# Three to four residual buffers and a post-norm traced in two parts, in a fp32 trunk of two layers

## The chip, the cores and the metric

The kernel runs on one core of one Trainium2 chip. The metric is the device time of one execution in microseconds. The times of the kernel before are 2248.75, 2250.59 and 2251.07 us, median 2250.59.

## The reference

A sequence of 1024 tokens of width 1024 passes through two layers in float32. The first has an attention mixer (eight banded softmax heads and eight stick-breaking heads), the second a gated linear recurrence. Every layer ends with a SwiGLU feed-forward part (FFN) of inner width 2816, and every sub-layer is wrapped in two RMS norms:

```python
def rmsnorm(x, g):
    y = x * lax.rsqrt(jnp.mean(x * x, axis=-1, keepdims=True) + RMS_EPS)
    return y * g
def swiglu(h, w_gate, w_up, w_down):
    return (jax.nn.silu(h @ w_gate) * (h @ w_up)) @ w_down
# each sub-layer f (mixer, FFN):
x = x + rmsnorm(f(rmsnorm(x, g_pre)), g_post)
```

Both mixers end in a product with a 1024 x 1024 matrix, `... @ w_out`.

## The kernel before

Tokens are handled in eight row blocks of 128. PE (the matrix engine) multiplies in float32 by splitting each operand into a high and a low part and adding three products. ACT (scalar engine) makes the high part by a cast, DVE (vector engine) the low part by a subtraction. POOL computes the small per-row numbers of the norms, SP issues the DMAs in the order of its queue. The program is written stage by stage; the framework's scheduler then fixes the order of every engine's instructions at build time, and each engine runs its list in that order. `issue_after(x)` adds the condition that an instruction is placed after x. It takes the data's own dependences for granted, and the buffers too: a tile with `bufs=n` shares n places, and its next user waits until the oldest one is done.

The stages, in order: attention, the output projection of the attention layer, its FFN in two stages (`gate_up`, `down`), the recurrent mixer, its output projection, and again `gate_up` and `down`.

**Output projection** (`out_product`). Row blocks 0 to 2, then 3 to 5 are summed in six PSUM banks over the eight slices of the inner dimension (L462 is its matmul). Then blocks 6 and 7 follow one by one. Each block's result goes through `norm`: `post_norm` squares the two halves of the PSUM result on ACT (L175 in `rstd`), POOL makes the factor rs from the sums (L177 adds the halves, L178 scales and adds eps, L179 takes the power -1/2), DVE multiplies by the gain (L223) and adds the result to the residual x (L226). The new x is stored, and `pre_norm` makes the next stage's input: square x (L175), factor, scale (L200, ACT), eight transposes on PE (L208, into tiles `pst`), and `take` of `HiddenS`, which copies (L85) and casts (L96) the transposed block and forms its four sums (L89).

**`gate_up`** multiplies the normed input by the gate and up matrices in Strassen form: seven products (`A11`, `A12`, `S2`, `S3`, `S1`, `S4`, `A22`) of half-size operands (L549 to L551 are its three matmuls). The weights' operands `q` are split in `load` (L529, L530; sums at L536 to L542). The very first Strassen product is done in two halves: `early`, columns of row blocks 0 to 3, while blocks 5 to 7 are still being normed, and `late` for blocks 4 to 7. L566 is the copy of the first product.

**`down`** multiplies by the down matrix in a similar form: sums p1, p6, p7, p5, p4, whose operands are loaded in pairs (`raw`) and split at L624/L625 (L629 to L631 are its matmuls). With p4 the second half of the rows (r = 1) is complete, and its four blocks are normed while p3 and then the `b21` products run (their activations `act` are cast at L740, their weights come from L731). The first half's blocks (r = 0) are normed last. In the last layer these post-norms write the output.

## Time and profile before

| | |
|---|---|
| median of three runs | 2250.59 us |
| the profiled execution | 2252.08 us |
| its span in the trace | 2250.3 us |
| PE busy | 2204.5 us (98%) |
| DVE busy | 1537.2 us (68%) |
| ACT busy | 1146.9 us (51%) |
| POOL busy | 220.5 us (10%) |
| mean granted PE clock | 0.992 |

The stages by the trace, with PE's busy time in each:

| stage | from, us | to, us | PE busy, us |
|---|---|---|---|
| attention | 0 | 495 | 486.13 |
| output projection, attention layer | 495 | 609 | 113.53 |
| `gate_up` 0 | 609 | 1015 | 401.08 |
| `down` 0 | 1015 | 1262 | 241.42 |
| recurrent mixer | 1262 | 1500 | 234.67 |
| output projection, recurrent layer | 1500 | 1588 | 87.53 |
| `gate_up` 1 | 1588 | 1990 | 398.03 |
| `down` 1 | 1990 | 2250.3 | 242.09 |

Busy time of an engine is the time in which one of its instructions runs; a stretch in which PE is idle or runs at a lower granted clock is time that the kernel could lose. Times in the trace are counted from the span's start.

### The profile page before, as it was taken

What the parts mean: (1) busy time and instruction counts of PE and PEld (TensorE: products, weight loads), DVE (VectorE), ACT (ScalarE), POOL (GpSimd) and SP (SyncE); (2) the same over time, 40 slices, a digit from 0 to 9 for tenths busy, and PEclk for the clock granted to TensorE, in tenths of its full rate; (3) what the DMA queues carried; (4) which work ended last, traced back from release to release, by engine and by line L of the source; (5) the groups of instructions that cost most, each with busy time, mean ns of one, the idle gap of its engine ahead of it and who ended that gap; (6) DMA issues with size and microseconds to landing.
All of it is one profiled execution on the core that took longest, in us unless ns stands there. A gap on an engine that the chain in (4) does not pass through costs nothing. (4 is left out here: it accounts for less than half of the span.)

```text
span 2250.3 us, 30764 instructions
## 1 busy us (share of the span) xinstructions
PE 2204.5 (98%) x11166; PEld 1804.5 (80%) x11166; DVE 1537.2 (68%) x2504; ACT 1146.9 (51%) x2132; POOL 220.5 (10%) x474
## 2 busy tenths in 40 slices
PE   8999999999999999999999999999999999999997
PEld 8888888878678888888887777887788888888875
DVE  5776765464677767676867677436887767769665
ACT  4545455465765454432536576537755454425433
POOL 2111212131100000000001232102000000000010
PEclk9999999999999999999999999999999999999998
DMA  5101011125623323245558511358233323337466
GB/s 171 44 29 34 24 43 46 55 98 156 223 85 113 116 90 122 89 131 183 173 157 255 141 57 47 95 183 273 71 117 108 122 90 116 96 117 264 130 206 187
DMA packets 187132, 273.13 MB, mean 121 GB/s; under 512 B 13922, under 2 KB 115298, under 8 KB 186979
## 3 DMA queue, kind: packets, MB, share of 16 engines
q1 hardware_dynamic: 186338, 269.06, 38.1%
q10 hardware_dynamic: 640, 2.10, 0.3%
q8 instruction: 88, 1.44, 0.3%
q14 instruction: 66, 0.53, 0.1%
HBM read 205.57 MB, written 65.54 MB: 120 GB/s over the span
## 5 line engine op out<-in xcount | busy, mean ns | idle before, releaser
L549 PE MATMUL ps<-hS,q 128*128 128x512 f32 (+1 forms) x1288 | 490.5, 382 | 3.0 <-ACT hS L96 2.9
L550 PE MATMUL ps<-hS,q 128*128 128x512 f32 (+1 forms) x1288 | 490.6, 381 | 0.2 <-DVE hS L89 0.2
L551 PE MATMUL ps<-hS,q 128*128 128x512 f32 (+1 forms) x1288 | 489.1, 381 | 0.0
L530 DVE TENSOR_TENSOR q<-raw,q 128x512 fp32r<-128x512 f32 x308 | 204.4, 686 | 180.8 <-ACT q L529 180.4
L549 PEld LDWEIGHTS ps<-hS,q 128*128 128x128 f32 x1288 | 242.8, 189 | 50.1 <-ACT hS L96 4.1
L550 PEld LDWEIGHTS ps<-hS,q 128*128 128x128 f32 x1288 | 243.7, 189 | 47.2 <-DVE hS L89 0.7
L551 PEld LDWEIGHTS ps<-hS,q 128*128 128x128 f32 x1288 | 243.6, 189 | 45.8
L529 ACT CAST q<-raw 128x512 fp32r<-128x512 f32 x308 | 176.9, 615 | 157.3 <-DVE raw L538 137.1
L630 PE MATMUL ps<-o,o 128*128 128x512 f32 x616 | 241.2, 392 | 2.4 <-DVE o L625 2.3
L631 PE MATMUL ps<-o,o 128*128 128x512 f32 x616 | 238.6, 392 | 0.5 <-DVE o L741 0.5
L629 PE MATMUL ps<-o,o 128*128 128x512 f32 x616 | 222.0, 395 | 8.9 <-ACT o L740 5.9
L518 ACT ACTIVATE raw<-raw,gcol 128x256 f32<-128x256 f32 x352 | 150.2, 498 | 157.2 <-DMA raw<-in_ffn_w_up_dram 83.1
L624 ACT CAST o<-raw 128x512 fp32r<-128x512 f32 x206 | 123.9, 621 | 197.2 <-PE ps L631 60.5
L625 DVE TENSOR_TENSOR o<-raw,o 128x512 fp32r<-128x512 f32 x206 | 137.9, 688 | 66.2 <-ACT o L624 65.2
L178 POOL TENSOR_SCALAR rs<-ss 128x1 f32<-128x1 f32 x64 | 30.2, 472 | 1266.5 <-ACT junk L175 1169.1
L629 PEld LDWEIGHTS ps<-o,o 128*128 128x128 f32 x616 | 116.4, 189 | 37.7 <-ACT o L740 8.0
L155 DVE TENSOR_TENSOR wlo<-raw,whi 128x1024 fp32r<-128x1024 f32 x76 | 92.9, 1223 | 67.5 <-ACT whi L154 66.4
L630 PEld LDWEIGHTS ps<-o,o 128*128 128x128 f32 x616 | 116.4, 189 | 28.0 <-DVE o L625 3.9
L631 PEld LDWEIGHTS ps<-o,o 128*128 128x128 f32 x616 | 116.3, 189 | 24.9 <-DVE o L741 0.9
L154 ACT CAST whi<-raw 128x1024 fp32r<-128x1024 f32 x76 | 79.8, 1052 | 53.0 <-PE ps L166 20.2
L369 ACT COPY pt<-tr 128x512 f32<-128x512 f32 (+1 forms) x128 | 65.5, 527 | 78.9 <-PE tr L365 78.3
L165 PE MATMUL psq<-hT,whi 128*128 128x512 f32 x256 | 101.2, 395 | 1.1 <-DVE v L264 1.1
(194 smaller groups left out, 4281.1 us busy)
## 6 DMA issues: line engine op xcount, KB each, us to landing
raw<-in_ffn_w_down_dram SPq DMA_DIRECT2D x96, 256.0 KB, 4.3
raw<-in_ffn_w_gate_dram SPq DMA_DIRECT2D x44, 512.0 KB, 4.2
raw<-in_ffn_w_up_dram SPq DMA_DIRECT2D x44, 512.0 KB, 4.4
gS<-c SPq DMA_DIRECT2D x88, 256.0 KB, 3.7
raw<-gS SPq DMA_DIRECT2D x88, 256.0 KB, 2.9
gA<-c SPq DMA_DIRECT2D x66, 256.0 KB, 3.3
raw<-in_attn_w_in_dram SPq DMA_DIRECT2D x24, 512.0 KB, 4.1
raw<-in_attn_w_out_dram SPq DMA_DIRECT2D x24, 512.0 KB, 4.2
```

The source lines that it names most:

```text
L165: nc.tensor.matmul(ps, wh[:, kt, cols], hh[:, kt, :], start=kt == 0, stop=False)
L518: nc.scalar.activation(raw[:, i], raw[:, i], AF.Copy, scale=gain[:, 4 * k + i:4 * k + i + 1])
L529: self.last = nc.scalar.copy(t[:, 0], src).ins
L530: nc.vector.tensor_tensor(t[:, 1], src, t[:, 0].bitcast(F32), op=ALU.subtract)
L549: nc.tensor.matmul(ps, a[:, 0, kt, :], bh, start=kt == 0, stop=False)
L550: nc.tensor.matmul(ps, a[:, 0, kt, :], bl, start=False, stop=False)
L551: nc.tensor.matmul(ps, a[:, 1, kt, :], bh, start=False, stop=kt == 3)
L624: nc.scalar.copy(t[:, 0], src)
L625: tt(t[:, 1], src, t[:, 0].bitcast(F32), op=ALU.subtract)
L629: nc.tensor.matmul(ps, a[0], b[:, 0], start=first, stop=False)
L630: nc.tensor.matmul(ps, a[0], b[:, 1], start=False, stop=False)
L631: nc.tensor.matmul(ps, a[1], b[:, 0], start=False, stop=last)
```

## The change

Four things change.

1. The residual tile x has three buffers instead of two in the output projections and the first `down`. The last `down` takes it from a pool of its own, `late`, with four. In the output projection block 5's x lies in a tile that the first activations also use, and the other activations have two buffers instead of three.
2. `post_norm` is split: a first part (load of x, squares, factor, multiplication by the gain) and a rest (residual, store, pre-norm, transposes). In the output projection the first parts of three blocks are written ahead of their rests, and likewise for blocks 6 and 7.
3. `rstd` scales inside the square and adds eps to the first half's sum, so that one POOL operation less follows the second half's square.
4. Placement: block 6's `take`, and three of the splits for the first gate matrix, are placed after block 7's last square and multiplication (`last_m`). The S2 product of the early half is placed after block 6's last transpose (`turned[6]`), its A22 product after block 7's (`turned[7]`).

```diff
 def rstd(self, pool, parts, junk):
-        for p, o in zip(parts, ss):
-            self.squared = nc.scalar.activation(junk, p, AF.Square, accum_out=o).ins
-        if len(parts) == 2:
-            nc.gpsimd.tensor_tensor(ss[0], ss[0], ss[1], op=ALU.add)
-        nc.gpsimd.tensor_scalar(rs, ss[0], 1.0 / D, EPS, op0=ALU.mult, op1=ALU.add)
+        eps = EPS
+        for i, (p, o) in enumerate(zip(parts, ss)):
+            self.squared = nc.scalar.activation(junk, p, AF.Square, scale=D ** -0.5, accum_out=o).ins
+            if i < len(parts) - 1:
+                nc.gpsimd.tensor_scalar(o, o, eps, None, op0=ALU.add)
+                eps = o
+        nc.gpsimd.tensor_scalar(rs, ss[-1], eps, None, op0=ALU.add)
         nc.gpsimd.tensor_tensor(rs, rs, self.neghalf, op=ALU.pow)
...
+    def behind(self, instructions):
+        with ExitStack() as c:
+            for i in instructions:
+                c.enter_context(self.tc.issue_after(i))
+            yield
...
-        sink.take(t, pst, h, pool)
+        with self.behind(behind):
+            sink.take(t, pst, h, pool)
...
-        x = pool.tile([P, D], F32, tag="nx", bufs=2, name=self.uid("x"))
+        if x is None:
+            x = pool.tile([P, D], F32, tag="nx", bufs=3, name=self.uid("x"))
...
-        nc.vector.scalar_tensor_tensor(x, mg, rs, x, op0=ALU.mult, op1=ALU.add)
...
+        self.last_m = [self.squared, scaled]
+        def rest(behind=()):
+            nc.vector.scalar_tensor_tensor(x, mg, rs, x, op0=ALU.mult, op1=ALU.add)
...
+                self.pre_norm(pool, x, mg, None, sink, t, self.psum_t, behind)
+        return rest
...
 def out_product(...):
+            x = self.apool.tile([P, 1152], F32, tag="first", name=self.uid("x"))[:, :D] if t == 5 else None
+            return self.post_norm_of(ms, mg, x_src, x_dst, t, gpost, sink, ap, x)
...
-            for t in range(3):
-                norm(t0 + t, pst[t])
+            for rest in [norm(t0 + t, pst[t]) for t in range(3)]:
+                rest()
...
-            norm(6 + t, ps)
+            rests.append(norm(6 + t, ps))
+        for rest, b in zip(rests, (self.last_m, ())):
+            rest(b)
...
 def gate_up(...):
             split("S2", a11)
-            split("S3", a21)
-            split("S1", a22)
-            tt(a12, a12, a11, op=ALU.subtract)
-            split("S4", a12)
+            with self.behind(behind):
+                split("S3", a21)
+                split("S1", a22)
+                tt(a12, a12, a11, op=ALU.subtract)
+                split("S4", a12)
...
-            tt(u2, product(new(), q["S2"], 4, cols), s1, op=ALU.add)
+            with self.behind([self.turned[6]] if first else ()):
+                p6 = product(new(), q["S2"], 4, cols)
+            tt(u2, p6, s1, op=ALU.add)
...
-            tt(u3, u3, product(new(), q["A22"], 6, cols), op=ALU.subtract)
+            with self.behind([self.turned[7]] if first else ()):
+                p4 = product(new(), q["A22"], 6, cols)
+            tt(u3, u3, p4, op=ALU.subtract)
...
 def down(...):
-            with make_sink() as sink:
+            with make_sink() as sink, self.pool("late", "right") as late:
+                if sink is not None:
+                    late = None
...
+                    x = late.tile([P, D], F32, tag="nx", bufs=4, name=self.uid("x")) if late else None
+                    self.post_norm(ms, mg, x_src, x_dst, (r, a), gpost, sink, ap, x)
```

The scheduler's order of PE at the handover from the attention layer's output projection to `gate_up`, before: `pst` are the transposes (those of `mg_6459` are block 6's, of `mg_6522` block 7's), `ps_6690` is the last product ahead of S2, `ps_6703` is S2 and `ps_6718` is S3 of the early half; `ps_6779` begins the late half.

```order
L551 MATMUL ps_6690<-hS_5636,q_6651 128x256
L549 MATMUL ps_6703<-hS_5640,q_6652 128x256
...
L551 MATMUL ps_6703<-hS_5640,q_6652 128x256
L549 MATMUL ps_6718<-hS_5640,q_6653 128x256
L550 MATMUL ps_6718<-hS_5641,q_6653 128x256
L208 MATMUL pst_6481<-ident,mg_6459 128x128 x4
L208 MATMUL pst_6486<-ident,mg_6459 128x128 x4
L551 MATMUL ps_6718<-hS_5640,q_6653 128x256
...
L208 MATMUL pst_6544<-ident,mg_6522 128x128 x4
L208 MATMUL pst_6549<-ident,mg_6522 128x128 x4
L549 MATMUL ps_6779<-hS_5636,q_6650 128x256
```

The same place on PE, after (the numbers in the names differ, and lines move: L549 becomes L587, L208 becomes L220; `mg_6457` is block 6, `mg_6489` block 7, `ps_6701` is S2 and `ps_6730` S1):

```order
L589 MATMUL ps_6688<-hS_5636,q_6649 128x256
L220 MATMUL pst_6511<-ident,mg_6457 128x128 x4
L220 MATMUL pst_6516<-ident,mg_6457 128x128 x4
L587 MATMUL ps_6701<-hS_5640,q_6650 128x256
...
L587 MATMUL ps_6730<-hS_5640,q_6652 128x256
L220 MATMUL pst_6542<-ident,mg_6489 128x128 x4
L588 MATMUL ps_6730<-hS_5641,q_6652 128x256
L220 MATMUL pst_6547<-ident,mg_6489 128x128 x4
L589 MATMUL ps_6730<-hS_5640,q_6652 128x256
```

Block 6's transposes move from behind 14 products, and block 7's from the end of the early half into its S1 product, 32 rows earlier.

On ACT at the same place, before: `x_6460` is block 6's residual sum, whose square begins its pre-norm, `mg_6364` is block 5, `pst_6386` and `pst_6391` its transposes.

```order
L85 COPY mg_6319<-pst_6341 128x512
L175 ACTIVATE mg_6459,ss_6476<-x_6460 128x1024
L85 COPY mg_6319<-pst_6346 128x512
L529 CAST q_6652<-raw_6638 128x512
...
L96 CAST hS_5638<-mg_6319 128x4x64
L200 ACTIVATE mg_6459<-x_6460,rs_6475 128x1024
L529 CAST q_6655<-raw_6644 128x512
L96 CAST hS_5640<-tf_6353 128x16x64
L85 COPY mg_6364<-pst_6386 128x512
L85 COPY mg_6364<-pst_6391 128x512
```

ACT after, where `x_6458` is block 6's residual sum, `mg_6300` is block 5, `ps_6472` the second half of block 7's PSUM result:

```order
L85 COPY mg_6300<-pst_6384 128x512
L178 ACTIVATE junk_6492,ss_6497<-ps_6472 128x512
L85 COPY mg_6300<-pst_6389 128x512
L178 ACTIVATE mg_6457,ss_6506<-x_6458 128x1024
L566 CAST q_6651<-raw_6636 128x512
L566 CAST q_6652<-raw_6642 128x512
L566 CAST q_6653<-raw_6642 128x512
L605 COPY first_6673<-ps_6674 128x256
L96 CAST hS_5636<-mg_6300 128x8x64
L96 CAST hS_5638<-mg_6300 128x4x64
L212 ACTIVATE mg_6457<-x_6458,rs_6505 128x1024
L178 ACTIVATE mg_6489,ss_6537<-x_6490 128x1024
```

The square and the scaling of block 6 stood ahead of both copies of block 5; now the copies stand ahead of the square, and three casts, a copy and two more casts ahead of the scaling.

On SP in the last `down`, before: `x_19347` and `x_19360` are the residuals of the third and fourth block of r = 1, `x_19713` and `x_19781` of the first two of r = 0, `raw_19612` to `raw_19657` are the b21 weights, and `act` the last activations.

```order
L228 DMA out_dram<-x_19321 64x1024
L192 DMA x_19347<-xs_91 64x1024
...
L192 DMA x_19360<-xs_91 64x1024 x2
...
L731 DMA raw_19612<-in_ffn_w_down_dram 128x512 x2
L192 DMA x_19713<-xs_91 64x1024 x2
L731 DMA raw_19621<-in_ffn_w_down_dram 128x512 x2
L731 DMA raw_19630<-in_ffn_w_down_dram 128x512 x2
L192 DMA act_19672<-gA_1_14669 128x3x128
L192 DMA act_19730<-gA_1_14669 128x4x128
L192 DMA x_19781<-xs_91 64x1024 x2
```

SP after: `x_19324` to `x_19363` are the four residuals of r = 1, `x_19716` to `x_19920` those of r = 0, `raw_19615` to `raw_19633` the first b21 weights; `raw_19401` is the second pair of p3's operands.

```order
L196 DMA x_19350<-xs_91 64x1024 x2
L196 DMA x_19363<-xs_91 64x1024 x2
L768 DMA raw_19401<-gS_1_1_14659 128x512
...
L251 DMA out_dram<-x_19324 64x1024
L196 DMA x_19716<-xs_91 64x1024 x2
...
L196 DMA x_19784<-xs_91 64x1024 x2
L196 DMA x_19852<-xs_91 64x1024 x2
L196 DMA x_19920<-xs_91 64x1024
L778 DMA raw_19615<-in_ffn_w_down_dram 128x512 x2
...
L778 DMA raw_19633<-in_ffn_w_down_dram 128x512 x2
L196 DMA act_19675<-gA_1_14669 128x3x128
L196 DMA act_19733<-gA_1_14669 128x4x128
```

The loads of residuals move ahead: two of r = 1 to before p3's second pair, all four of r = 0 to before the last activations.

More of the change, by code (lines that the diff above doesn't have):

```diff
@@ L192, in load, with pre_norm @@
             return self.nc.sync.dma_start(dst, src)
[L194 removed]
+    @contextmanager
+    def behind(self, instructions):
[3 more added lines that the diff above has]
+            yield
+    def pre_norm(self, pool, x, h, g, sink, t, psum, behind=()):
         nc = self.nc
@@ L222, in post_norm @@
         for c, m in ms:
-            nc.vector.tensor_tensor(mg[:, c], m, gpost[:, c], op=ALU.mult)
+            scaled = nc.vector.tensor_tensor(mg[:, c], m, gpost[:, c], op=ALU.mult).ins
         if mg is not ms[0][1]:
             rs = self.rstd(pool, [m for _, m in ms], junk)
-        nc.vector.scalar_tensor_tensor(x, mg, rs, x, op0=ALU.mult, op1=ALU.add)
-        for k, (d, s) in enumerate(rows(t, x_dst)):
-            (nc.scalar if k and sink is None else nc.sync).dma_start(s, x[d, :])
-        if sink is not None:
-            self.pre_norm(pool, x, mg, None, sink, t, self.psum_t)
+        self.last_m = [self.squared, scaled]
+        def rest(behind=()):
+            nc.vector.scalar_tensor_tensor(x, mg, rs, x, op0=ALU.mult, op1=ALU.add)
+            for k, (d, s) in enumerate(rows(t, x_dst)):
+                (nc.scalar if k and sink is None else nc.sync).dma_start(s, x[d, :])
+            if sink is not None:
+                self.pre_norm(pool, x, mg, None, sink, t, self.psum_t, behind)
+        return rest
     def attention(self, x_src, w_in, bias_t, o_dst, hT):
@@ L473, in out_product @@
             for kt in kts:
-                pool, bufs = (self.apool, 1) if t0 == 0 and kt == kts[0] else (ap, 3)
-                a = act(kt, t0, 3, pool, bufs)
+                if t0 == 0 and kt == kts[0]:
+                    first = self.apool.tile([P, 1152], F32, tag="first", name=self.uid("first")).rearrange(
+                        "p (a b) -> p a b", a=3)
+                    a, ah, al = first[:, 0], first[:, 1].bitcast(F32R), first[:, 2].bitcast(F32R)
+                    nc.sync.dma_start(a, aT[kt][:, 0:3 * P])
+                else:
+                    a = act(kt, t0, 3, ap, 2)
+                    ah, al = (ap.tile([P, 384], F32R, tag=n, bufs=3, name=self.uid(n)) for n in ("ah", "al"))
                 wh, wl = self.split(wv[kt], 2, 512)
-                ah, al = (pool.tile([P, 384], F32R, tag=n, bufs=bufs, name=self.uid(n)) for n in ("ah", "al"))
                 nc.scalar.copy(ah, a)
@@ L493, in out_product @@
             rows.append(raw)
-            acts.append(act(kt, 6, 2, ap, 3, ("act", "ah", "al")[i % 3]))
+            acts.append(act(kt, 6, 2, ap, (3, 3, 2)[i % 3], ("ah", "al", "act")[i % 3]))
+        rests = []
         for t in range(2):
@@ L498, in out_product, with load @@
                 matmuls(ps, [(acts[i][:, t * P:(t + 1) * P], rows[i])], i == 0, i == KT - 1)
-            norm(6 + t, ps)
+            rests.append(norm(6 + t, ps))
+        for rest, b in zip(rests, (self.last_m, ())):
+            rest(b)
     def gate_up(self, ap, hS, wg, wu, gain, gO):
         nc = self.nc
-        def load(w, j, tags, after=None):
+        def load(w, j, tags, after=None, behind=()):
             a = []
@@ L557, in blocks, with strassen @@
             return [ap.tile([P, 512], F32, tag="c", bufs=11, name=self.uid("c")) for _ in range(4)]
-        def strassen(c, q, cols):
+        def strassen(c, q, cols, first=False):
             s1, u2, u3, c22 = c
@@ L574, in strassen @@
             tt(u2, product(new(), q["S4"], 2, cols), u2, op=ALU.add)
-            tt(u3, u3, product(new(), q["A22"], 6, cols), op=ALU.subtract)
+            with self.behind([self.turned[7]] if first else ()):
+                p4 = product(new(), q["A22"], 6, cols)
+            tt(u3, u3, p4, op=ALU.subtract)
         full, early, late = slice(0, 512), slice(0, 256), slice(256, 512)
         for j in range(NF // 2):
-            qg = load(wg, j, ["w"] * 7, self.last if j == 1 else None)
+            qg = load(wg, j, ["w"] * 7, self.last if j == 1 else None, () if j else self.last_m)
             if j == 0:
                 first = self.main.tile([P, 4, 256], F32, tag="w", bufs=8, name=self.uid("first"))
-                strassen([first[:, i] for i in range(4)], qg, early)
+                strassen([first[:, i] for i in range(4)], qg, early, True)
                 cg = blocks()
```

12 lines of the change are left out of this document (7 added, 5 removed).

## The prediction

> **What bounds the kernel now.** I read the page's busy shares first, then the waits of the matrix engine (PE), then PE's own instructions around its longest waits, then stretches cut where the clock steps. The first row caps everything: PE is busy for 2204.5 of 2250.3 us, so all its idle time is some 46 us. The waits (total us, times, longest) say which of it the change can touch:
>
> ```profile
> PE 2204.5 (98%) x11166; PEld 1804.5 (80%) x11166; DVE 1537.2 (68%) x2504; ACT 1146.9 (51%) x2132; POOL 220.5 (10%) x474
> ...
> PE ps L629 <- ACT o L740: 5.9, 4, 2.5
> PE pst L208 <- ACT mg L200: 5.1, 2, 2.9
> PE ps L462 <- ACT junk L175: 0.9, 2, 0.5
> ```
>
> The second lies where an output projection hands over to the FFN, the first in the two down stages. L462 is the output projection waiting for a PSUM bank until the squares of the post-norm have read it. The handover in PE's timeline (start, us, operation, idle before it and its releaser), first the attention layer's, then the recurrent layer's:
>
> ```profile
> 608.90 0.69 PE L549 MATMUL ps<-hS,q 128*128 128x256 f32 x1
> ...
> 610.37 1.04 PE L208 MATMUL pst<-ident,mg 128*128 128x128 f32 x8
> ...
> 614.47 0.28 PE L549 MATMUL ps<-hS,q 128*128 128x256 f32 x1
> 614.59 0.28 PE L550 MATMUL ps<-hS,q 128*128 128x256 f32 x1
> 615.45 1.14 PE L208 MATMUL pst<-ident,mg 128*128 128x128 f32 x8 [0.58 <-ACT mg L85]
> ...
> 625.02 1.71 PE L208 MATMUL pst<-ident,mg 128*128 128x128 f32 x8 [2.92 <-ACT mg L200]
> 628.06 0.80 PE L549 MATMUL ps<-hS,q 128*128 128x256 f32 x2 [1.32 <-ACT hS L96]
> ...
> 633.25 0.74 PE L549 MATMUL ps<-hS,q 128*128 128x256 f32 x4
> ...
> 1587.49 0.69 PE L549 MATMUL ps<-hS,q 128*128 128x256 f32 x1
> ...
> 1588.96 1.03 PE L208 MATMUL pst<-ident,mg 128*128 128x128 f32 x8
> ...
> 1593.30 1.04 PE L208 MATMUL pst<-ident,mg 128*128 128x128 f32 x8
> ...
> 1601.98 1.09 PE L208 MATMUL pst<-ident,mg 128*128 128x128 f32 x8 [2.14 <-ACT mg L200]
> 1604.50 0.51 PE L549 MATMUL ps<-hS,q 128*128 128x256 f32 x2 [1.43 <-ACT hS L96]
> 1605.23 0.58 PE L550 MATMUL ps<-hS,q 128*128 128x256 f32 x1 [0.22 <-DVE hS L89]
> ...
> 1609.69 0.74 PE L549 MATMUL ps<-hS,q 128*128 128x256 f32 x4 [0.18 <-ACT hS L96]
> ```
>
> The x8 rows are the transposes of row blocks 5, 6 and 7; between them run the products of the early half (blocks 0 to 3). The late half starts at 628.06, and 633.25 is where all of late's first two sums are issued: my finish line in both versions, since PE's order is the same from there on. The waits also cost clock. Cut at steps of 3.41 us (columns: stretch, length, PE busy, ..., granted clock, DMA share, GB/s):
>
> ```profile
> 621.95:625.36 3.41, 0.49 (x5) 0.34 (x4) 3.41 (x8) 2.82 (x4) 0.93 (x2) 1.00 0.37 154
> 625.36:628.77 3.41, 2.09 (x9) 1.48 (x7) 2.37 (x7) 2.55 (x5) 0.00 (x0) 0.50 0.01 2
> 628.77:632.18 3.41, 3.41 (x17) 3.39 (x17) 3.04 (x6) 0.53 (x2) 0.00 (x0) 0.50 0.00 0
> ...
> 1598.14:1601.55 3.41, 1.70 (x15) 1.50 (x13) 3.41 (x9) 2.86 (x4) 0.93 (x2) 1.00 0.37 154
> 1601.55:1604.96 3.41, 1.55 (x10) 1.16 (x10) 2.88 (x7) 2.58 (x6) 0.00 (x0) 1.00 0.00 0
> 1604.96:1608.38 3.42, 3.20 (x15) 3.15 (x15) 3.12 (x7) 0.75 (x1) 0.00 (x0) 0.50 0.00 0
> ```
>
> A stretch with PE busy for 0.49 or 1.55 us is followed by one at half clock; one with 1.70 is not. What each handover loses is thus, in the attention layer, 0.58 + 2.92 + 1.32 = 4.82 us idle plus half of the 2.09 + 3.41 us run at half clock, 2.75: 7.6 us. In the recurrent layer it is 2.14 + 1.43 + 0.22 + 0.18 = 3.97 plus half of 3.20: 5.6 us. Without losses PE would need 633.25 - 608.90 - 7.6 = 16.8 us and 1609.69 - 1587.49 - 5.6 = 16.6 us from its first Strassen product to the finish line.
>
> **The change at the two handovers.** By PE's order (rows above), block 6's transposes move up by 14 products, ahead of the first S2 product, and block 7's move up by 32 rows, into the S1 product. At 0.12 us a product (614.47 to 614.59), PE arrives at block 6's transposes at 615.45 - 0.58 - 14 x 0.12 = 613.2 instead of 614.9, and has 16.8 - 4.3 = 12.5 us of work left to the finish line. What counts is when block 6 can be there. Before, ACT, DVE and POOL did this:
>
> ```profile
> 608.40 1.06 ACT L175 ACTIVATE mg<-x 128x1024 f32<-128x1024 f32 x1 [2.88 <-DVE x L226]
> 609.92 1.66 ACT L529 CAST q<-raw 128x512 fp32r<-128x512 f32 x3
> 611.49 0.92 ACT L96 CAST hS<-mg 128x512 fp32r<-128x512 f32 x2
> 612.32 1.15 ACT L200 ACTIVATE mg<-x,rs 128x1024 f32<-128x1024 f32 x1
> 614.82 1.06 ACT L85 COPY mg<-pst 128x512 f32<-128x512 f32 x2
> 616.36 0.38 ACT L566 COPY first<-ps 128x256 f32<-128x256 f32 x1
> ...
> 618.51 0.52 POOL L178 TENSOR_SCALAR rs<-ss 128x1 f32<-128x1 f32 x1
> 619.11 0.55 POOL L179 TENSOR_TENSOR rs<-rs,neghalf 128x1 f32<-128x1 f32 x1
> ```
>
> Block 6's square (608.40) ran ahead of block 5's copies. By ACT's new order it stands behind both of them, and they need block 5's transposes (610.37, first four done about 610.9). So: copy, a square of block 7's PSUM half, copy, at some 0.55 us each (two copies took 1.06), bring the square of block 6 to 612.6 instead of 608.4; it ends at 613.7. POOL's two operations (0.52 + 0.55 and a gap) give the factor at about 615.0. But ACT still has three casts (1.66), the copy of the first product (0.38, overlapping) and block 5's two casts (0.92) ahead of block 6's scaling: 613.7 + 2.7 = 616.4, plus 1.1 us, so the transposes can start at 617.5. PE idles from 613.2 to 617.5, 4.3 us, where before it idled 0.58.
>
> Block 7 is then no longer late: its square follows block 6's scaling, 617.5 to 618.5, POOL 1.1, scaling 1.1, transposes from about 620.8; PE reaches them 28 products after 618.3, at 621.7 or later. So the 2.92 goes. The late products need block 7's copies and casts; from transposes to 628.06 took 3.0 us before, two thirds of it at half clock, so about 625 after, while PE ends its early products only near 627 to 629: the 1.32 goes too. The 4.3 takes their place, with the clock: at these 3.41 us steps, 611.7 to 615.1 holds 1.5 us of PE work and the next stretch 1.0, both below 1.55, so half clock from 615.1 to 621.95, of which PE works 4.45 us and loses 2.2. Finish line: 617.5 + 12.5 + 2.2 = 632.2 against 633.25, a gain of 1.1 us.
>
> The recurrent layer has the same order, and in it block 6's transposes did not wait before. Block 5's transposes stand at 1588.96, 978.6 later, so block 6's come at 617.5 + 978.6 = 1596.1, and the finish line at 1596.1 + 12.5 + 2.2 = 1610.8 against 1609.69: 1.1 us lost. Together **0**. Where the steps fall relative to the program is not fixed, so the clock term of each is open between 0 and two stretches' halves, 3.4 us: together -4.4 to +2.4 us. I keep 2.2, the value of the phase shown.
>
> A rule against the change: the Trainium skill, "TensorE: Matmul & The Clock Gate", section "Why this matters for your kernels", asks for no idle gaps above about 3 us between matmul bursts, since one window of idle halves the clock. By it only the new 4.3 us waits would cost clock, about one stretch's half (1.7 us) each, and the sum would be 1 us lower; in this trace a wait of 2.14 us, below that, already was followed by half clock.
>
> **PSUM and the norm's operations.** Tracing all three first parts ahead of the rests puts squares and multiplications, which free PSUM, ahead of other work: I take the 0.9 us of L462 as won (bounds 0 and -0.9). The first norm part's addition leaves the chain: one POOL operation less after the last square. In the handovers this is inside the sums; at the program's end it is on the path. The scale inside the square rides in an instruction that runs anyway: 0.
>
> ```profile
> 2242.81 0.19 POOL L177 TENSOR_TENSOR ss<-ss,ss 128x1 f32<-128x1 f32 x1 [3.56 <-ACT junk L175]
> 2243.09 0.19 POOL L178 TENSOR_SCALAR rs<-ss 128x1 f32<-128x1 f32 x1
> ```
>
> The two start 0.28 us apart: **-0.3**.
>
> **Down stages.** The last down stage, in PE's, DVE's and ACT's timelines and one stretch:
>
> ```profile
> 2204.86 0.50 PE L629 MATMUL ps<-o,o 128*128 128x512 f32 x1 [1.47 <-ACT o L624]
> 2209.62 0.80 PE L629 MATMUL ps<-o,o 128*128 128x512 f32 x1 [2.48 <-ACT o L740]
> ...
> 2187.44 1.28 DVE L226 SCALAR_TENSOR_TENSOR x<-m,rs,x 128x1024 f32<-128x1024 f32 x1 [5.71 <-DMA x<-xs]
> ...
> 2208.95 0.62 ACT L740 CAST o<-act 128x512 fp32r<-128x512 f32 x1 [0.94 <-DMA act<-gA]
> ...
> 2182.00:2214.00 32.00, 27.04 (x99) 20.38 (x98) 18.89 (x28) 13.35 (x24) 0.00 (x0) 0.84 1.01 293
> ```
>
> Here DMA is the limit: share 1.01 at 293 GB/s. With four residual buffers, SP issues all four loads of the first half's residuals before its second pair of sums (1 MB moved out of the saturated stretch), so DVE's 5.71 us wait goes. It then issues the second half's four loads (2 MB) so early that all of them precede the two activation loads behind 2209.62, where 0.5 MB did. Net, 0.5 MB more stands ahead of those: at 293 GB/s 1.7 us later. Against it stand the stretch's small waits, 32.00 - 27.04 - 1.47 - 2.48 = 1.0 us, of which I count 0.8 as following from DVE's delayed queue. I take **+0.9**. Bounds: all idle of the stretch goes with the half clock behind it, -7.1 (worked out below), or 1.5 MB weighs in full, +5.1, and a half-clock stretch more, 1.7. In the first down stage each residual is loaded one step earlier with the same bytes in all: 0, between -1.7 and +1.7 by the same 0.5 MB.
>
> **Sum.** 0 - 0.9 - 0.3 + 0.9 = -0.3 us on the profiled 2252.08, which is its span of 2250.3 plus 1.8 outside; that execution is 1.5 above the median of 2250.59. On the median: **2250.3 us**. About 0.2%, 4.5 us, is what a measurement of this kernel can tell from no change; this is far within it.
>
> **Rivals.** *Both stalls really vanish.* If block 6's scaling is ready by 613.2 and 1591.6, both handovers lose nothing: -7.6 - 5.6 = -13.2, so 2237.1. For it: block 7's chain, the one waited for, does get shorter. Against it: ACT runs in order, and block 5's copies, which stand ahead, cannot start before 610.9.
>
> *The residual buffers free the tail.* If the early loads fill time in which DMA was idle, all 4.96 us of idle in that stretch go. Its clock of 0.84 means 0.16 x 32 x 2 = 10.2 us at half speed, three steps of 3.41: the first follows an earlier stall and stays, the other two hold the 2.48 us of idle and lose half of the remaining 4.3, 2.1. That is 7.1, in place of +0.9: 2250.3 - 8.0 = 2242.3. Against it: the bytes ahead of the activations grow.
>
> *Slower: residuals ahead of the last activations.* If the megabyte loaded earlier is no help, because the first store and not the bytes sets when the saturated stretch begins, the 1.5 MB of second-half residuals delay what releases 2209.62 by 5.1 us, and one more step runs at half clock (1.7): +6.8 instead of +0.9, 2256.2. It decides once those activations land more than 2 us later than before. For it: share 1.01. Against it: 1 MB leaves the same stretch.
>
> **Chances.** The forecast with its open terms (2246 to 2253) 0.54; stalls vanish in whole or large part 0.12; tail freed 0.14; slower case 0.20. The range leaves out the first rival and the far end of the slower one: 2242 to 2256. Faster by over 0.2% (below 2246.1): 0.12 + 0.13 + 0.03 = 0.28. Slower (above 2255.1): 0.13 of the slower case and 0.02: 0.15. The rest, 0.57, lies within.
>
> **What the changed profile would show.** Right: PE waits of some 4 us for ACT's scaling ahead of block 6's transposes, in both handovers, none ahead of block 7's; two stretches near half clock after the former and none at the late half's start; no L462 waits; no DVE wait for x near 2187, and PE's wait for the activations cast near 2210 longer by 1 to 2 us. Wrong: transposes of block 6 without a wait, or saturation by DMA that ends before PE needs the last activations.

## The result, and the profile after

The changed kernel takes 2265.67 us (median of four runs, 2264.17 to 2267.77) against 2250.83 for the kernel before: a ratio of 1.0066 with a 95% interval of 1.0049 to 1.0084. It is 15 us slower, 9.7 us beyond the upper end of the range. Its profiled execution took 2267.77 us, the longest of the four, with a span of 2266.0. Of all the runs below one execution, of e1, fell in a slow state (3131.88 us at a granted clock of 0.653), and the ratios are worked out without it (e1's median is 2254.79 without it). The waits of PE in the trace after (us in total, times, longest):

```profile
PE 2212.2 (98%) x11166; PEld 1807.3 (80%) x11166; DVE 1537.7 (68%) x2504; ACT 1150.1 (51%) x2132; POOL 240.1 (11%) x474
...
PE pst L220 <- ACT mg L212: 10.3, 2, 5.2
PE ps L487 <- ACT junk L178: 4.2, 2, 2.1
PE ps L487 <- ACT ah L510: 1.9, 1, 1.9
```

L220 are the transposes, L212 the scaling ahead of them, L487 the output projection's matmuls and L178 the squares. The 10.3 us are the forecast waits for block 6. The wait for squares was to vanish, but grew from 0.9 to 4.2 us, and it moved: before, its two parts of 0.47 us stood at 548.65 and 1527.26, at the start of blocks 3 to 5, where PE no longer waits; now it stands ahead of block 6's sums. The wait for `ah`, the cast of the activations, is new. Where they stand in PE's timeline (start, us, operation, idle before and releaser):

```profile
583.74 2.84 PE L487 MATMUL ps<-raw,act 128*128 128x512 f32 x6 [2.11 <-ACT junk L178]
612.66 0.68 PE L587 MATMUL ps<-hS,q 128*128 128x256 f32 x1
622.10 1.97 PE L220 MATMUL pst<-ident,mg 128*128 128x128 f32 x8 [5.16 <-ACT mg L212]
637.12 0.74 PE L587 MATMUL ps<-hS,q 128*128 128x256 f32 x4 [0.32 <-ACT hS L96]
...
1508.32 0.75 PE L487 MATMUL ps<-whi,ah 128*128 128x512 f32 x1 [1.93 <-ACT ah L510]
1568.63 5.83 PE L487 MATMUL ps<-raw,act 128*128 128x512 f32 x9 [2.09 <-ACT junk L178]
1599.25 0.68 PE L587 MATMUL ps<-hS,q 128*128 128x256 f32 x1
1608.69 1.54 PE L220 MATMUL pst<-ident,mg 128*128 128x128 f32 x6 [5.15 <-ACT mg L212]
1623.65 0.74 PE L587 MATMUL ps<-hS,q 128*128 128x256 f32 x4 [0.32 <-ACT hS L96]
```

Cutting each trace at the same instructions of PE gives the time of each stretch. "Projection" runs from the first matmul of an output projection (511.15 before, 512.67 after; 1489.88 and 1493.99) to the first Strassen product (608.90 and 612.66; 1587.49 and 1599.25). "Handover" runs from there to the finish line of the prediction, "middle" from the first finish line to the second projection, "end" from the second finish line to the end of the span. All in us of one profiled execution:

| kernel | attention | projection 1 | handover 1 | middle | projection 2 | handover 2 | end | span |
|---|---|---|---|---|---|---|---|---|
| before | 511.15 | 97.75 | 24.35 | 856.63 | 97.61 | 22.20 | 640.61 | 2250.3 |
| after | 512.67 | 99.99 | 24.46 | 856.87 | 105.26 | 24.40 | 642.35 | 2266.0 |
| difference | +1.5 | +2.2 | +0.1 | +0.2 | +7.7 | +2.2 | +1.7 | +15.7 |

So 9.9 of the 15.7 us lie inside the two output projections, to which the prediction gave -0.9. Nearly half of the second one's loss is clock, as the stretches around its two new waits show (length, PE busy, ..., granted clock, DMA share, GB/s):

```profile
1506.00:1510.00 4.00, 2.07 (x6) 1.39 (x5) 1.29 (x3) 1.97 (x3) 0.00 (x0) 0.80 1.03 409
1510.00:1514.00 4.00, 4.00 (x15) 3.16 (x15) 1.05 (x1) 1.04 (x2) 0.00 (x0) 0.77 0.87 295
...
1566.00:1570.00 4.00, 1.91 (x6) 0.79 (x5) 3.97 (x6) 2.05 (x6) 0.67 (x3) 0.98 1.02 380
1570.00:1574.00 4.00, 4.00 (x7) 1.66 (x6) 3.16 (x4) 3.22 (x9) 3.55 (x5) 0.59 1.04 407
```

A clock of 0.80 and 0.77 in two stretches of 4 us, and of 0.98 and 0.59, each stand for one step of 3.4 us at half speed, some 1.6 us lost. The first projection's wait of 2.11 us was not followed by a half clock. Cut at the steps of 3.41 us, it is divided between two of them, and the one that holds most of it still has PE busy for 1.64 us:

```profile
579.98:583.39 3.41, 1.64 (x8) 1.03 (x6) 2.29 (x4) 1.45 (x2) 0.00 (x0) 1.00 0.96 313
```

In projection 2 the waits add 1.93 + 2.09 - 0.47 and the clock 3.3, which is 6.9 of the 7.7; the rest I did not trace.

Why the squares are late can be read on DVE and ACT where block 3's sums end. First the kernel before, DVE and then ACT, then the kernel after, DVE and then ACT:

```profile
575.28 1.23 DVE L89 TENSOR_TENSOR hS<-tf,hS 128x1024 fp32r<-128x1024 f32 x1 [0.23 <-ACT hS L96]
576.89 4.09 DVE L223 TENSOR_TENSOR mg<-ps,g 128x512 f32<-128x512 f32 x6 [0.38 <-PE ps L462]
...
577.61 0.60 ACT L175 ACTIVATE junk<-ps 128x512 bf16<-128x512 f32 x1 [2.36 <-DVE mg L223]
```

```profile
577.65 0.76 DVE L89 TENSOR_TENSOR tf<-mg 128x256 f32<-128x256 f32 x2
...
581.13 1.23 DVE L89 TENSOR_TENSOR hS<-tf,hS 128x1024 fp32r<-128x1024 f32 x1 [1.12 <-ACT hS L96]
582.28 3.67 DVE L243 TENSOR_TENSOR mg<-ps,g 128x512 f32<-128x512 f32 x6
...
583.00 0.60 ACT L178 ACTIVATE junk<-ps 128x512 bf16<-128x512 f32 x1 [1.89 <-DVE mg L243]
```

Each square starts just after the multiplication of the same PSUM half: 576.89 + 0.68 and 577.61 before, 582.28 + 0.68 and 583.00 after. Before, block 2's take (L89) was finished when the sums ended, and DVE waited for PE. After, the whole take of block 2, from 577.65 to 582.36, stands ahead of block 3's multiplication, and PE waits for the bank until 583.74.

### The profile page after: what moved, and what is told of

Same layout as the page of the kernel before. It is cut to its first block, busy times and chain, and to the rows that moved or that the text cites. A ratio compares the mean times of both kernels' runs of the same rounds, so it can differ in the third digit from the quotient of the medians.

```text
span 2266.0 us, 30755 instructions
## 1 busy us (share of the span) xinstructions
PE 2212.2 (98%) x11166; PEld 1807.3 (80%) x11166; DVE 1537.7 (68%) x2504; ACT 1150.1 (51%) x2132; POOL 240.1 (11%) x474
## 3 DMA queue, kind: packets, MB, share of 16 engines
q8 instruction: 88, 1.44, 0.3%
## 5 line engine op out<-in xcount | busy, mean ns | idle before, releaser
L587 PE MATMUL ps<-hS,q 128*128 128x512 f32 (+1 forms) x1288 | 490.9, 382 | 0.6 <-ACT hS L96 0.6
L587 PEld LDWEIGHTS ps<-hS,q 128*128 128x128 f32 x1288 | 243.4, 189 | 47.4 <-ACT hS L96 1.1
L182 POOL TENSOR_SCALAR rs<-ss 128x1 f32<-128x1 f32 x44 | 27.0, 613 | 1241.1 <-ACT junk L178 1180.6
```

Source lines behind the costliest of these rows:

```text
L587: nc.tensor.matmul(ps, a[:, 0, kt, :], bh, start=kt == 0, stop=False)
```

## The experiments

Each stretch of every kernel's profiled execution, cut at the same instructions as above; "time" and "before" are medians of the runs, with the ratio to the kernel before on the same chip and its 95% interval. A profiled execution lies between 3.8 us below (e1) and 2.0 us above (e11) its kernel's median:

| run | projection 1 | handover 1 | projection 2 | handover 2 | end | time | before | ratio |
|---|---|---|---|---|---|---|---|---|
| e1 | 97.71 | 23.07 | 99.04 | 22.84 | 640.79 | 2254.97 | 2250.17 | 1.0021 [1.0012, 1.0031] |
| e2 | 96.91 | 25.24 | 96.77 | 26.31 | 641.37 | 2254.80 | 2250.17 | 1.0023 [1.0014, 1.0032] |
| e3 | 100.22 | 25.18 | 103.51 | 25.01 | 642.33 | 2265.58 | 2250.17 | 1.0069 [1.0052, 1.0086] |
| e4 | 99.72 | 23.84 | 103.18 | 24.06 | 640.36 | 2264.56 | 2250.17 | 1.0062 [1.0047, 1.0077] |
| e5 | 97.73 | 25.89 | 97.60 | 25.73 | 641.46 | 2258.83 | 2252.83 | 1.0026 [1.0017, 1.0036] |
| e6 | 96.91 | 24.97 | 98.40 | 25.60 | 641.10 | 2259.76 | 2252.83 | 1.0034 [1.0021, 1.0047] |
| e7 | 97.77 | 23.74 | 97.63 | 23.09 | 643.11 | 2255.72 | 2252.83 | 1.0013 [1.0004, 1.0022] |
| e8 | 97.73 | 26.82 | 97.59 | 24.42 | 640.54 | 2258.60 | 2252.83 | 1.0023 [1.0013, 1.0032] |
| e9 | 97.85 | 26.95 | 99.36 | 26.72 | 641.57 | 2261.37 | 2250.62 | 1.0040 [1.0026, 1.0053] |
| e10 | 97.77 | 23.03 | 97.64 | 22.71 | 642.01 | 2251.35 | 2250.62 | 1.0003 [0.9994, 1.0012] |
| e11 | 97.72 | 24.63 | 97.56 | 23.25 | 641.81 | 2253.81 | 2250.62 | 1.0008 [1.0000, 1.0017] |
| e12 | 97.71 | 21.46 | 97.61 | 21.10 | 638.78 | 2245.97 | 2250.62 | 0.9981 [0.9971, 0.9991] |

How far the same code differs from one execution to the next is seen in after, e3 and e4, which share the code of both projections: 99.7 to 100.2 and 103.2 to 105.3 us. After and e4 share the handovers too: 24.46 and 23.84, 24.40 and 24.06. The end, too, differs by 1.5 us among after, e1, e2 and e3 (640.79 to 642.35), which share its code.

**e1: blocks 0 to 5 normed one after the other.**

```diff
-            for rest in [norm(t0 + t, pst[t]) for t in range(3)]:
-                rest()
+            for t in range(3):
+                norm(t0 + t, pst[t])()
```

> The changed kernel, but for row blocks 0 to 5 each block's post-norm runs whole, block after block, as before; blocks 6 and 7 stay in two parts. Theory: writing three first parts ahead of three rests delays the transposes and the take of blocks 1 and 2, and in DVE's in-order list the take of block 2 then stands ahead of block 3's gain multiplication, on which the squares that free PSUM wait. It predicts that PE's waits for junk ahead of block 6's sums (2.11 and 2.09 us) fall to 0 to 0.5, the half clock behind the second (1.6) goes, and the kernel takes 2260 to 2262 us instead of 2265.7. Rival: the squares are late because loads come late with two activation buffers; then both waits stay near 2 us and the time at 2265 to 2267.

Measured 2254.97 us, 5 us lower than the theory's range. The wait for squares ahead of block 6's sums is gone, and projection 1 is back at 97.71; projection 2 keeps a wait for the activations:

```profile
1500.31 0.50 PE L487 MATMUL ps<-whi,ah 128*128 128x512 f32 x1 [1.18 <-ACT ah L510]
1530.55 0.50 PE L487 MATMUL ps<-whi,ah 128*128 128x512 f32 x1 [0.33 <-ACT junk L178]
```

The two-part order in the loops over three blocks is thus needed for the wait. It gave more than was asked of it: the wait for activations is shorter and no half clock follows it in this trace, and the handovers fell as well (23.07 and 22.84). There block 6's wait is as long as in the changed kernel (5.20 and 5.19 us); PE works for 3.7 and 3.2 us at half clock instead of 5.7 and 5.5, which is 1.0 and 1.2 us, and depends on where the steps fall, and the wait of 0.32 us at the finish line is gone.

**e2: the old buffers in the output projections.**

```diff
-            x = self.apool.tile([P, 1152], F32, tag="first", ...)[:, :D] if t == 5 else None
+            x = ap.tile([P, D], F32, tag="nx", bufs=2, name=self.uid("x"))
...
-                    a = act(kt, t0, 3, ap, 2)
+                    a = act(kt, t0, 3, ap, 3)
```

> The changed kernel, but the output projections have their old buffers: two for the residual x, also for block 5, and three for the activations. Theory: at the start of the recurrent layer's output projection SP issues four residual loads (2 MB) ahead of weights where it issued two, and the third activation load waits for a buffer; that gives PE's wait of 1.93 us there for the cast of the activations and half clock behind it (1.7). It predicts both gone, the attention's end as before (1.5 us earlier), and 2260 to 2262 us. Rival: the wait comes from the recurrent mixer's end being late or from the half clock alone; then it stays at 1.5 to 2 us and the time at 2264 to 2267. The waits for junk ahead of block 6 stay near 2.1 us if the first experiment's theory holds, and vanish if late loads cause them.

Measured 2254.80 us, again lower than expected. The wait for `ah` is gone, as the theory said. But so is the wait for squares, though the two-part order is kept: the projections take 96.91 and 96.77 us, 0.8 us less than before. So the late squares need both parts of the change together. With two residual buffers the scheduler writes block 3's first multiplication ahead of the last piece of block 2's take, and one bank is free in time. The handovers got longer instead:

```profile
619.16 1.11 PE L220 MATMUL pst<-ident,mg 128*128 128x128 f32 x4 [7.73 <-ACT mg L212]
```

**e3: no placement.** The `behind` orders are taken out of `take`, of the splits and of the S2 and A22 products.

> The changed kernel without the placement: block 6's take and the splits are not put behind block 7's squares, and the S2 and A22 products not behind the transposes. From the first Strassen product to the finish line (the third sum of the late half) the changed kernel takes 24.46 us in the attention layer and 24.40 in the recurrent one, the kernel before 24.35 and 22.20. Theory: PE's 5.2 us wait for block 6 is made by the placement, and goes; waits for block 7 as in the kernel before come back: 24 and 22.2 us, so 2263 to 2264 us in all. Rival: the wait comes from ACT's order that the two-part norm makes; then 5 us of wait for block 6 stay and the time at 2265 to 2267.

Measured 2265.58 us, where the rival put it, but not for the rival's reason. Block 6's wait falls from 5.16 to 0.70 us, as the theory said; the time comes back as waits for block 7 and for the casts of the late half, and the handovers take 25 us:

```profile
626.31 1.09 PE L220 MATMUL pst<-ident,mg 128*128 128x128 f32 x8 [0.70 <-ACT mg L212]
629.96 1.14 PE L220 MATMUL pst<-ident,mg 128*128 128x128 f32 x8 [2.43 <-ACT mg L85]
633.84 0.79 PE L587 MATMUL ps<-hS,q 128*128 128x256 f32 x2 [2.73 <-ACT hS L96]
```

The placement moves the wait to block 6. The 0.6 to 0.7 us a handover by which e3 is longer are hardly more than two executions of the same code differ by (0.6 and 0.3 above), so its worth stays open; it is not what costs 15 us.

**e4: old buffers in the down stages.** The pool `late` and the third buffer go; two residual buffers in both.

> The changed kernel, but both down stages have two residual buffers, as before. From the recurrent handover's finish line to the end of the span the changed kernel takes 642.3 us, the kernel before 640.6. Theory: the early residual loads delay what PE waits for in the last down stage by 1.7 us net; undone, that stretch takes 640.3 to 640.8 and the kernel 2263.5 to 2264.5 us. Rival: the four buffers are neutral and the difference is from the phase of the clock steps; then 2265 to 2267.

Measured 2264.56 us, just above the theory's range, with 640.36 us for the end. The medians differ by 1.1 us, less than the run-to-run spread of either, so this run alone decides nothing; e7 does.

**e5: the edits of e1 and e2 together.**

> The changed kernel with both edits of the first two experiments: blocks 0 to 5 normed one after the other, and the output projections' old buffers. Left of the change: blocks 6 and 7 in two parts, the placement, the squares' scale and one POOL operation less, the down stages' buffers. Theory (either edit alone breaks the bunching): the output projections take 97 to 98 us each, the handovers 23 us each as in the first experiment, so the kernel 2249 to 2252 us, level with before. Rival: the handover of the first experiment owed its shorter time to the early residuals; then the handovers take 25 to 26 us as in the second and the kernel 2254 to 2257.

The rival is right in the handovers: 25.89 and 25.73 us. In all it takes 2258.83 us, above both ranges and 6 us above the kernel before. The projections are back at 97.73 and 97.60. Most of what is left of the loss is block 6's wait, 7.61 us here (the down stages' buffers, still in, are e7's subject). Why it is longer than in e1 was not traced:

```profile
621.46 1.97 PE L220 MATMUL pst<-ident,mg 128*128 128x128 f32 x8 [7.61 <-ACT mg L212]
```

**e6: two residual buffers, but two for the activations too.** As e2, with `act(kt, t0, 3, ap, 2)` and the shared tile for the first activations kept.

> The changed kernel with two residual buffers in the output projections (block 5's x among them), but still only two activation buffers. Theory: the residual buffers are what matters; with two, block 2's sum waits for block 0's to be stored, the three rests do not bunch, and fewer loads run ahead of the weights: no wait for junk ahead of block 6's sums, the wait for ah near 1508 at most 0.5 us, 2253 to 2257 us. Rival: the activation buffers are what matters: the wait for ah of 1.2 to 1.9 us stays, and with it half clock, and the time is 2258 to 2267.

Measured 2259.76 us, in the rival's range. It splits the two effects: no wait for squares (96.91), so the residual buffers make that one, and the wait for activations stays, so their two buffers, or the shared tile of the first activations that goes with them, make this one. No half clock follows it in this trace:

```profile
1505.53 0.50 PE L487 MATMUL ps<-whi,ah 128*128 128x512 f32 x1 [1.33 <-ACT ah L510]
```

**e7: the kernel before with the down stages' buffers alone.**

> The kernel before with only the down stages' buffers changed (three residuals in the first, four from a pool of their own in the last). Theory: early residuals cost what they delay, so from the recurrent handover's finish line to the end 641.3 to 642.5 us where before takes 640.6, and 2251 to 2253 us in all. Rival: neutral, 640.2 to 641 and 2249 to 2251. A third outcome is a gain: DVE's wait of 5.7 us for x goes and with it the small waits of PE after 2187, 638 to 640 and 2247 to 2249.

Measured a ratio of 1.0013, 2.9 us slower, and 643.11 us for the end where before took 640.61. PE's longest wait in the last down stage, and DVE ahead of it:

```profile
2184.71 0.79 PE L631 MATMUL ps<-o,o 128*128 128x512 f32 x1 [3.29 <-DVE o L626]
...
2178.78 1.28 DVE L227 SCALAR_TENSOR_TENSOR x<-m,rs,x 128x1024 f32<-128x1024 f32 x1
2179.97 2.35 DVE L224 TENSOR_TENSOR m<-m,g 128x1024 f32<-128x1024 f32 x2
2182.77 1.28 DVE L227 SCALAR_TENSOR_TENSOR x<-m,rs,x 128x1024 f32<-128x1024 f32 x1 [0.44 <-POOL rs L179]
2183.97 1.29 DVE L626 TENSOR_TENSOR o<-raw,o 128x512 fp32r<-128x512 f32 x2
```

With every residual at hand, DVE's list has a residual sum, two gain multiplications and another sum in a row ahead of the low part that p3 needs: PE waits 3.29 us where it waited 1.85; in the changed kernel it is 2.77, at 2197.88. The wait for the cast of the last activations, which the forecast expected to grow, is 0.46 (2.48 before, 1.04 in the changed kernel). So the buffers cost here, and by this trace through DVE's order and not through the activations' load; no run changed that order alone.

**e8: block 6's square first.** Built on e5 with old down buffers: block 5's `take` is placed behind block 6's square, the splits also behind block 6's scaling.

> Blocks 0 to 5 normed one after the other, old buffers everywhere, blocks 6 and 7 in two parts with the placement, and one order more: block 5's take stands behind block 6's square, and the three splits also behind block 6's scaling. In ACT's list block 6's square is then ahead of block 5's copies and its scaling ahead of the casts. Theory: PE's 5.2 us wait for block 6 is that order, and falls to about 1; block 7's transposes wait 0 to 2; the handovers take 19.5 to 21.5 us each and the kernel 2243 to 2247 us. Rival: block 7 is as late as before, and PE's wait only moves on: 3 to 4 us ahead of block 7's transposes, handovers of 22 to 23.5 and 2249 to 2252 us.

Measured 2258.60 us; both ranges missed. The wait for block 6 stayed 5.64 us:

```profile
618.88 1.97 PE L226 MATMUL pst<-ident,mg 128*128 128x128 f32 x8 [5.64 <-ACT mg L216]
...
613.06 0.60 ACT L179 ACTIVATE junk<-ps 128x512 bf16<-128x512 f32 x1 [1.89 <-DVE mg L255]
...
614.37 1.05 ACT L179 ACTIVATE mg<-x 128x1024 f32<-128x1024 f32 x1
615.40 1.06 ACT L85 COPY mg<-pst 128x512 f32<-128x512 f32 x2
```

Here block 6's square is ahead of block 5's copies and still starts at 614.37, since it stands behind both squares of block 7, and these wait for DVE's multiplication; its scaling then waits for POOL until 617.68. So what holds block 6 back is not the copies alone, as I had it, but by this trace also block 7's first part, which the two-part order puts ahead; no run took that away alone.

**e9: block 2's take behind block 3's squares.** One order added to the changed kernel; the rest of block 2 keeps its transposes, and its `take` is traced after block 3's first part, behind its square and multiplication.

> The changed kernel with one order more: the take of block 2 (and of block 2 alone) is placed behind block 3's squares and gain multiplications. Theory: PE's 2.1 us waits for junk ahead of block 6's sums come from DVE's list, where block 2's take stands ahead of block 3's multiplication; with it behind, both waits fall below 0.5 us, the attention layer's output projection takes 97 to 98 us instead of 99.99, the recurrent one 99 to 102 instead of 105.26 (the wait for activations of 1.2 to 1.9 us and its half clock stay), and the kernel 2258 to 2262 us. Rival: the squares are late for another reason (the sums end late, ACT is busy): the waits stay above 1.5 us and the time at 2264 to 2268.

Measured 2261.37 us, within the theory's range. Projection 1 takes 97.85 us, projection 2 99.36, and neither waits for squares ahead of block 6's sums. This shows what makes the wait for squares. The time is not won with it in the attention layer: projection and handover together take 124.80 us where the changed kernel takes 124.45, since block 6's wait grows to 8.06 us. In the recurrent layer they take 126.08 instead of 129.66, of which 0.5 is a shorter wait for activations and 1.7 the half clock behind it, which this execution does not have:

```profile
622.63 1.76 PE L221 MATMUL pst<-ident,mg 128*128 128x128 f32 x7 [8.06 <-ACT mg L213]
```

**e10: the kernel before, with the three splits behind block 7's first part.**

> The kernel before with one order of the change alone: the S3, S1 and S4 splits of the first gate matrix are placed behind block 7's squares and gain multiplications. Theory: DVE is full at the handover, so block 7's chain starts earlier by what is put behind it (two splits and a difference, 1.9 us), block 6's chain keeps its place ahead, and the waits ahead of block 7's transposes (2.92 and 2.14 us) fall to about 1; the handovers take 22 to 23 and 20 to 21.5 us instead of 24.35 and 22.20, the kernel 2246 to 2249 where before takes 2250.5. Rival: the splits become late for PE's S3 product, or the takes of blocks 4 and 5 move back instead; then handovers of 24 to 26 us and 2250 to 2255.

Measured 2251.35 us, a ratio that holds 1. Block 7's transposes no longer wait, as the theory said, but the casts of the late half do (1.43, 1.85 and 1.62 us), which is the rival's kind of loss:

```profile
624.44 0.50 PE L559 MATMUL ps<-hS,q 128*128 128x256 f32 x2 [1.43 <-ACT hS L96]
626.80 0.41 PE L560 MATMUL ps<-hS,q 128*128 128x256 f32 x1 [1.85 <-DVE hS L89]
632.81 0.74 PE L559 MATMUL ps<-hS,q 128*128 128x256 f32 x4 [1.62 <-ACT hS L96]
```

**e11 and e12: the shorter norm with the splits, and alone.** Both take `rstd` of the change; e12 has nothing else of it.

> The previous kernel with the change's scaled squares too (one POOL operation less behind the last square). Theory: 0.3 us less at the end and up to 0.3 in each handover than the kernel with the splits alone, 2245.5 to 2248.5. Rival: POOL's time is set by what DVE does beside it (operations of 0.28 us took 1.3 us beside DVE's residual sums), and nothing changes beyond 0.5 us.

> The kernel before with the scaled squares and the shorter POOL chain alone. Theory: -0.3 us at the end and at most as much in each handover: 2249.5 to 2250.5 where before takes 2250.5. Rival: the scheduler, seeing a shorter chain, writes another order in the output projections (36 instructions of PE move), and the handovers change by up to 2 us either way: 2247 to 2254.

e11 took 2253.81 us, above its theory's range and no better than e10. e12 took 2245.97 us, a ratio of 0.9981 with an interval of 0.9971 to 0.9991: faster than both kernels, by 4.7 us than before and about 20 than the change. The rival's mechanism fits: from the projections on, the engines' orders differ from those of the kernel before. Block 6's residual sum now runs on DVE at 603.83 instead of 607.08, its square on ACT at 605.14 instead of 608.40, and block 7's transposes wait 1.38 us instead of 2.92. From 624 to 632 the granted clock is 0.81 and 0.76 in two stretches of 4 us, where the kernel before has 0.67 and 0.50: one step at half clock instead of two, in one execution each. The handovers take 21.46 and 21.10 us.

```profile
603.83 1.28 DVE L229 SCALAR_TENSOR_TENSOR x<-mg,rs,x 128x1024 f32<-128x1024 f32 x1 [0.46 <-POOL rs L182]
...
605.14 1.06 ACT L177 ACTIVATE mg<-x 128x1024 f32<-128x1024 f32 x1 [1.98 <-DVE x L229]
...
623.24 0.98 PE L211 MATMUL pst<-ident,mg 128*128 128x128 f32 x7 [1.38 <-ACT mg L203]
```

Whether that order can be had with the rest of the change was not tried.

## Why the prediction was wrong

*The step that failed* is "PSUM and the norm's operations". It took the 0.9 us of L462 as won, with bounds 0 and -0.9, since first parts ahead of rests free PSUM sooner. That is true within three blocks: the two waits of 0.47 us are gone. But the rests that are put off have to go somewhere, and they go to the next three blocks: block 2's take lands on DVE ahead of block 3's multiplication. The term measured +1.6 in the first projection (2.11 - 0.47) and, with the clock, +3.3 in the second. e9, which moves only this, takes the waits away, and so does e1, which undoes the two-part order of blocks 0 to 5; e2 and e6 show that three residual buffers are needed for them as well. Undoing either part, order (e1) or buffers (e2), brings back 10 of the 15 us. A bound below which nothing could be lost was given without regard to DVE's order at that place.

Not every wait that went was time won. From the projection's first matmul to block 6's transposes the changed kernel takes 109.4 us in the attention layer; e2, e5, e6 and e9, without the wait for squares, take 108.6 to 110.2, and only e1 and e8 are earlier (107.2 and 107.7). PE that does not wait in the projection waits longer for block 6 there. In the recurrent layer it is 114.7 against 106.1 to 111.7 in e1, e2, e5, e6, e8 and e9.

*The step that was left out* is the price of the activations' third buffer. The change's list names it, and no term did. It cost a wait of 1.93 us and a step at half clock at the start of the second projection, where DMA's share is 1.03; e6 keeps the wait and e2 is free of it. The first projection starts without such a wait. The step at half clock is this execution's: e3 and e4, with the same code there, wait 1.43 and 1.44 us, and no half clock follows.

*The handovers* were right in kind: a wait for block 6 of 4 to 5 us (5.16 and 5.15), none for block 7 (628.94 and 1615.46 to 1616 start without one), none at the late half's start and 0.32 us at the finish line. In size they came 1.2 us and 1.1 us above the forecast of -1.1 and +1.1. The reason given for the wait was incomplete, as e8 shows: in ACT's order the squares of block 7 stand ahead too, and they wait for DVE's multiplication (0.64 us at 616.15 in the trace after):

```profile
615.37 0.68 DVE L243 TENSOR_TENSOR mg<-ps,g 128x512 f32<-128x512 f32 x1
...
616.15 0.60 ACT L178 ACTIVATE junk<-ps 128x512 bf16<-128x512 f32 x1 [0.64 <-DVE mg L243]
617.20 1.07 ACT L178 ACTIVATE mg<-x 128x1024 f32<-128x1024 f32 x1
...
620.89 1.16 ACT L212 ACTIVATE mg<-x,rs 128x1024 f32<-128x1024 f32 x1
```

With 3.76 us of lag at the first Strassen product, the forecast's 612.6 for this square is 616.4 and its 616.4 for the scaling 620.2; they came at 617.20 and 620.89.

*The clock* behind block 6's wait came as forecast, two steps of it at half speed:

```profile
620.00:624.00 4.00, 1.90 (x9) 1.90 (x10) 2.60 (x5) 4.00 (x8) 1.02 (x3) 0.62 0.81 272
624.00:628.00 4.00, 4.00 (x22) 4.00 (x21) 2.98 (x6) 2.96 (x6) 0.04 (x1) 0.53 0.37 123
```

The deficits, 0.38 and 0.47 of 4 us, make 6.8 us at half clock; PE works in it for about 5.7, so it loses 2.8, against 2.2 in the forecast. The forecast's reading of the steps, that 1.55 us of PE's work or less in one brings half clock in the next, fits here too: the steps that hold the waits of 1.93 and 2.09 us have PE busy for 1.48 and 1.32 us, the one at 579.98 for 1.64. For a step already at half clock it is too low: one with 2.09 us before, and one with 2.25 after, was followed by another. The last section counts these steps over all traces. On the rule of the Trainium skill that was weighed there ("TensorE: Matmul & The Clock Gate", "Why this matters for your kernels"), the trace after speaks as the one before did: waits of 1.93 and 2.09 us, below the page's 3 us, were followed by a step at half clock, and one of 2.11 us was not.

*The last down stage* was forecast at +0.9 - 0.3 and measured +1.7 between the two profiles, with an uncertainty of about 1.5 us by the repeats. e7 says that the buffers alone cost 2.9 us in the median (0.0004 to 0.0022 of the time, 0.9 to 5.0 us). The forecast's sign was right and its mechanism wrong: DVE's wait for x did go, but what took its place is, by e7's trace, DVE's own order, and not the load of the activations.

*The shorter norm* was put at -0.3; alone it measured -4.7 us (e12), and the scheduler's order changes with it; next to the moved splits it gained nothing (e11 against e10). What it is worth in the changed kernel no run tells.

*The attention's end*: 1.5 us are left. The five kernels with three residual buffers in the projections and their two-part form or not (after, e1, e3, e4, e9) reach the first projection at 512.7 on the mean, the eight with the old buffers (before, e2, e5, e7, e8, e10 to e12) at 511.3, spread over 2.7 and 1.8 us; e6, with two residual buffers and two for the activations, at 511.28. The orders of PE and DVE differ there, so part of it may be the change's; no run was made to settle it.

None of the three rivals named what happened.

## What to carry to other kernels

Work that is put off in one group of tiles is done in the next: when first parts are traced ahead of rests, look in the order of the busiest helper engine at the place where the next group's first part must start. Buffers that are given to one tile are taken from another, and each needs its own term, with the place where DMA is already full. And where a scheduler orders the program, an edit's own cost can be smaller than what the new order brings: one POOL operation less on the path, forecast at 0.3 us, moved this kernel by 4.7, and by nothing once three splits were placed elsewhere. A wait of PE ahead of a longer one may cost nothing: before it is counted as a loss, the time at which the longer one ends has to be asked for.

## What the runs showed of the hardware

A small operation of POOL can last until DVE's operation beside it is done. In the trace after, an addition on 128 numbers takes 0.22 us alone (at 623.17). All 17 additions of L180 (eps to the first half's sum) and L182 (the factor's sum) that begin beside a residual sum on DVE (`x`) end 0.08 to 0.15 us after that sum, and take up to 1.32 us. Beside DVE's multiplication out of PSUM (`mg<-ps,g`) it is otherwise: the four additions of L180 that begin there take 0.22 us. Both in one place:

```profile
585.59 0.22 POOL L180 TENSOR_SCALAR ss<-ss 128x1 f32<-128x1 f32 x1
586.01 1.28 POOL L182 TENSOR_SCALAR rs<-ss,ss 128x1 f32<-128x1 f32 x1 [0.20 <-ACT junk L178]
...
583.48 2.48 DVE L243 TENSOR_TENSOR mg<-ps,g 128x512 f32<-128x512 f32 x4
585.87 1.27 DVE L249 SCALAR_TENSOR_TENSOR x<-mg,rs,x 128x1024 f32<-128x1024 f32 x1
```

The forecast had counted 1.1 us for POOL's two operations ahead of block 6's scaling; they took 1.15 + 0.59 and the gaps, since the first (at 618.45) ran beside the residual sum at 618.24. And a square on ACT and the multiplication on DVE that reads the same half of a PSUM result were never seen at once: in none of the fourteen traces does a square begin before the multiplication has ended, and the closest begin 0.03 us after it. The traces name DVE's multiplication as what releases such a square (`<-DVE mg L243` above), so the program waits for it; what the chip would do without that wait, no run here tells.

In these traces PE's clock in a step of 3.41 us follows what PE did in the step before. Counted over all fourteen traces (without the first 20 us and the last steps): 51 steps at full clock had PE busy for at most 1.58 us, and half clock followed every one; from 1.59 to 2.03 us it followed 10 of 42; above that none. At half clock, 38 steps with at most 2.74 us busy were followed by another such step, and 61 of the 62 with 2.92 us or more by full clock. Products of 128x256 start 0.213 us apart at half clock and 0.12 at full (15 of them from 624.30 to 627.50, 5 from 613.41 to 614.01 after), so 2.74 and 2.92 us there are, as an estimate, the work of 1.5 and 1.6 us at full clock. So it is the work done in a fixed step, and not the length of one wait, that these counts follow.
